# One ones-product instead of two for the adaLN parts that only one stream uses

## The chip, the cores and the metric

The kernel runs on one NeuronCore of a Trainium2 chip. Its engines are TensorE (PE in the profile, with its weight loads shown apart as PEld), VectorE (DVE), ScalarE (ACT), GpSimd (POOL) and SyncE (SP), which issues nearly all transfers. The metric is the time of one execution on the device in microseconds (us): the median of several runs.

## The reference

The model is a two-layer backbone over 512 latent tokens and 256 context tokens, 1024 wide. Layer 0 mixes tokens with gated linear attention (GLA), layer 1 with an mLSTM; each is followed by a convolutional feed-forward network (FFN). Around every block stands an adaptive norm: six vectors of 1024 per layer and stream (shift, scale and gate for the mixer, then for the FFN), made from a conditioning vector. Cut to what matters here:

```python
for i in range(DEPTH):                      # DEPTH = 2
    need_ctx = i < DEPTH - 1
    mod_l = (silu(c)     @ ada_w[i] + ada_b[i])[:, None, :]   # latent stream, 6*1024
    mod_c =  silu(c_ctx) @ ada_w[i] + ada_b[i]                # context stream, 6*1024
    sh1_l, sc1_l, g1_l, sh2_l, sc2_l, g2_l = split(mod_l, 6)
    sh1_c, sc1_c, g1_c, sh2_c, sc2_c, g2_c = split(mod_c, 6)
    h_c = rmsnorm(ctx, norm_mix_g[i]) * (1 + sc1_c) + sh1_c
    h_l = rmsnorm(x,   norm_mix_g[i]) * (1 + sc1_l) + sh1_l
    ...                                     # mixer
    x = x + g1_l * o_l
    h_l = rmsnorm(x, norm_ffn_g[i]) * (1 + sc2_l) + sh2_l
    x = x + g2_l * conv_ffn(h_l, ...)
    if need_ctx:                            # layer 0 only
        ctx = ctx + g1_c * o_c
        h_c = rmsnorm(ctx, norm_ffn_g[i]) * (1 + sc2_c) + sh2_c
        ctx = ctx + g2_c * conv_ffn(h_c, ...)
return rmsnorm(x, final_norm_g)
```

In layer 1 the context stream is not needed behind the mixer's input, so of its six parts only 0 and 1 are wanted for both streams, and parts 2 to 5 (`g1`, `sh2`, `sc2`, `g2`) for the latent stream alone.

## The kernel before

All activations stay on the chip, with the 1024 channels in eight tiles of 128 partitions. Every big product runs as three fp32r products of split operands (`mm3`, lines 384 to 386: high by high, low by high, high by low), each weight tile arriving as a 512 KB transfer into one of three "stage" buffers (`load_w`, line 362), being cast on ACT (line 340) and its remainder taken on DVE (line 341).

The program goes through a start, the GLA heads, FFN 0 (lines 1568 on), the four mLSTM heads and FFN 1. The instruction order on each engine is set when the program is built, by a scheduler that knows what depends on what; on the chip each engine then works down its own list in that order and waits where a semaphore asks for it.

The adaptive norm's vectors for all but the first two parts are made by the generator `ada_seq`, whose steps are woven into other work. A part is 1024 columns of `ada_w`, taken as two halves of 512 columns, and a half as eight blocks of 128 rows (`k` = 0 to 7). For each block there is one transfer of 256 KB (line 540, tile `ast`, three buffers, issued two steps ahead), and then one step of accumulation over the row blocks: ACT writes the first product into a fresh tile `asum` (line 555), DVE adds the others to it (line 558). The tile `asum` has two buffers. When the eighth block is in, TensorE sums over the 128 partitions by a product with a matrix of ones, 32 columns wide, so that four of them fill the four column groups of the array (line 567); ACT copies the result (line 569, tile `aev`), TensorE transposes it (line 572) and DVE adds the bias into `mod` (line 575 for two streams, line 581 for one).

Where both streams are needed, a half has two sums of 512 columns and the four products take 256 columns each, with a copy of 256 columns and two transposes. Where one stream is needed, a half has one sum, the four products take 128 columns each, with a copy of 128 columns and one transpose.

Who takes the steps: in FFN 0 one step is taken behind each projection from block 4 on (`project`); part 2 of layer 1 falls there, around blocks 15 to 18. In the mLSTM stage, parts 3 to 5 are the side work of a `Filler`: `ml_scan`, one head's chain of small dependent steps, alternates with projections of the next head, and every 1.9 us of such filling, by the filler's own reckoning, one step of `ada_seq` is let in, up to a number of steps that is given per head.

The head's chain (lines 1425 to 1507) matters below. For ten steps, TensorE transposes a block of keys (`mkp`, line 1458), ACT scales it (`mktok`, line 1460), TensorE makes a state update (`mu`, line 1465) and DVE folds it into the state (`C`, line 1471). All of `mkp`, `mu`, the head's later outputs `num` and the transposes `hps` of the head before take their PSUM space from one ring of three buffers (`aux`). After the chain DVE multiplies the decays with the scores (`Wt`, line 1489).

In tile names, the digits behind `ast1_` and `asum0_1_` are part, half and row block: `ast1_413` is part 4, half 1, block 3. The digits behind `C`, `mu` and `mkp` are head, direction and block.

Of the kernel before, what the change touches and what calls it, by code (L numbers as in the profile page):

```python
# [16 lines left out]
F32 = mybir.dt.float32  # L17
# [3 lines left out]
AF = mybir.ActivationFunctionType  # L21
ALU = mybir.AluOpType
PSUM = bass.MemoryType.PSUM

P = 128
D = 1024
KT = D // P
# [273 lines left out]
class Body:  # L301
# [226 lines left out]
    def ada_seq(self, parts):  # L528
# [5 lines left out]
        nc = self.nc  # L534
# [10 lines left out]
        for i, (l, part, half, k) in enumerate(steps):  # L545
# [6 lines left out]
            if k == 0:  # L552
                acc = [self.pw.tile([P, 512], F32, tag="ada_sum", name=f"asum{s}_{nm}", bufs=2) for s in range(len(c))]
                for s in range(len(c)):
                    nc.scalar.activation(acc[s], st, AF.Copy, scale=c[s])  # L555
            else:
                for s in range(len(c)):
                    nc.vector.scalar_tensor_tensor(acc[s], st, c[s], acc[s], op0=ALU.mult, op1=ALU.add)  # L558
            yield 0.0
            if k < KT - 1:  # L560
                continue

            ps = self.ada_tile(f"ada{nm}")
            n = 256 if both else 128
            for j in range(4):
                x = acc[j % 2][:, j // 2 * n:j // 2 * n + n] if both else acc[0][:, j * n:j * n + n]
                nc.tensor.matmul(ps[32 * j:32 * j + 32, 0:n], self.ones, x, start=True, stop=True)
            ev = self.pw.tile([P, 256], F32, tag="adaev", name=f"aev{nm}", bufs=1)
            nc.scalar.copy(ev[:, :n], ps[:, :n])
            yield n / 474  # L570
            for i_ in range(n // P):
                nc.tensor.transpose(ps[:, 256 + i_ * P:256 + (i_ + 1) * P], ev[:, i_ * P:(i_ + 1) * P], self.ident)
            b = part * KT + half * 4
            if both:
                nc.vector.tensor_tensor(
                    self.mod[l][:, b:b + 4, :].rearrange("p (q i) s -> p q i s", i=2),
                    ps[:, 256:512].rearrange("p (i q s x) -> p q i s x", i=2, q=2, x=32)[:, :, :, :, 0],
                    self.adab[l][:, b:b + 4].rearrange("p (q i) -> p q i", i=2).unsqueeze(3).to_broadcast([P, 2, 2, 2]),
                    op=ALU.add)
            else:  # L580
                nc.vector.tensor_tensor(self.mod[l][:, b:b + 4, 0], ps[:, 256:384:32], self.adab[l][:, b:b + 4], op=ALU.add)
            if half and part in (1, 4):
                self.make_A(l, part // 4, 0, KT, 2 if both else 1)
            yield n / 1164
# [946 lines left out]
    def mlstm(self):  # L1531
        with ExitStack() as es:
# [16 lines left out]
            with self.tc.tile_pool(name="ml_b", bufs=1) as hpb:  # L1549
# [6 lines left out]
                for h in range(NH):  # L1556
# [12 lines left out]
                    fill = Filler(*fill, side=ada((15, 19, 18, 8)[h]))  # L1569
# [265 lines left out]
```

## Time and profile before

| | |
|---|---|
| median of 3 runs | 1616.74 us (1615.61 to 1618.33) |
| the profiled execution's own time | 1618.06 us |
| its span, first to last instruction | 1616.0 us, granted TensorE clock 0.998 |
| TensorE busy | 1595.1 us (99%), 9249 instructions |
| weight loads busy | 1378.6 us (85%) |
| VectorE busy | 1232.0 us (76%) |
| ScalarE busy | 679.2 us (42%) |
| GpSimd busy | 67.4 us (4%) |
| moved | 163.59 MB, 101 GB/s over the span |

The profile comes from one execution, which took 1618.06 us, 2.06 us more than its span; sums are made against the span, and then carried over to the median. In a row of the timeline stand the start and the length in us, the engine, the line, the operation with out<-in, and the shape; in brackets the idle time of the engine just before it and what ended it. Since matmuls are pipelined, what one costs on TensorE is read from the distance of two starts, not from its length.

### The profile page before, as it was taken

Reading aid. Unit: us, or ns where it says so; the run is one execution under the profiler, and the core shown is the slowest. Engines: PE = TensorE matmul, PEld = TensorE weight load, DVE = VectorE, ACT = ScalarE, POOL = GpSimd, SP = SyncE. Lnnn points to the kernel's source line nnn. Section 1 sums busy time; section 2 is a strip of 40 time slices with the busy share of each in tenths; the row PEclk is TensorE's granted clock in tenths of the full one; section 3 lists DMA queues with packets and bytes.
Section 4 is the critical chain, followed back from the end, with each engine's and each line's share of the span. In section 5 each row is a group of like instructions: output and inputs, shape, how many; then the busy total and the mean of one; then the engine's idle time right before and its main releaser. Section 6 shows DMA issues by size and latency. Waiting matters only on the chain. (4 is left out here: it accounts for less than half of the span.)

```text
span 1616.0 us, 23563 instructions
## 1 busy us (share of the span) xinstructions
PE 1595.1 (99%) x9249; PEld 1378.6 (85%) x9249; DVE 1232.0 (76%) x2123; ACT 679.2 (42%) x1149; POOL 67.4 (4%) x128
## 2 busy tenths in 40 slices
PE   7999999999999999999999999999999999999998
PEld 6789898889888888888888988888889888888887
DVE  5776988878985978695755678766778988877875
ACT  5673738435431314131321356545465422323334
POOL 0110101011000000000000020000001000000000
PEclk9999999999999999999999999999999999999999
DMA  9613453432240524251312205433340423223421
GB/s 304 183 51 101 128 154 93 133 96 82 88 124 27 149 74 118 65 169 51 100 53 63 57 27 151 137 112 104 98 118 14 123 89 99 85 79 100 117 79 53
DMA packets 178674, 163.59 MB, mean 101 GB/s; under 512 B 8924, under 2 KB 146788, under 8 KB 178564
## 3 DMA queue, kind: packets, MB, share of 16 engines
q1 hardware_dynamic: 178324, 161.97, 33.4%
q8 instruction: 72, 1.18, 0.3%
q14 instruction: 38, 0.31, 0.1%
q10 hardware_dynamic: 240, 0.13, 0.0%
HBM read 159.98 MB, written 2.10 MB: 100 GB/s over the span
## 5 line engine op out<-in xcount | busy, mean ns | idle before, releaser
L1648 DVE SCALAR_TENSOR_TENSOR acc<-gp,vt_f,acc 128x512 f32<-128x512 f32 x352 | 260.4, 748 | 4.6
L558 DVE SCALAR_TENSOR_TENSOR asum<-ast,sil,asum 128x512 f32<-128x512 f32 x224 | 163.8, 754 | 20.9 <-ACT asum L555 11.3
L384 PE MATMUL fd<-ahil,wh_d 128*128 128x512 f32 (+1 forms) x376 | 142.1, 378 | 0.6 <-DVE xl L629 0.5
L386 PE MATMUL fd<-ahil,wl_d 128*128 128x512 f32 (+1 forms) x376 | 141.7, 378 | 0.0
L385 PE MATMUL fd<-alol,wh_d 128*128 128x512 f32 (+1 forms) x376 | 141.3, 376 | 0.0
L629 DVE SCALAR_TENSOR_TENSOR xl<-fd,mod,xl 128x512 f32<-128x512 f32 (+1 forms) x128 | 90.8, 715 | 55.7 <-PE fd L386 55.1
L384 PE MATMUL fa<-hhi,wh_a 128*128 128x512 f32 x320 | 124.9, 390 | 0.0
L384 PE MATMUL fg<-hhi,wh_g 128*128 128x512 f32 x320 | 124.8, 390 | 0.0
L385 PE MATMUL fg<-hlo,wh_g 128*128 128x512 f32 x320 | 124.5, 389 | 0.0
L386 PE MATMUL fg<-hhi,wl_g 128*128 128x512 f32 x320 | 124.5, 389 | 0.0
L386 PE MATMUL fa<-hhi,wl_a 128*128 128x512 f32 x320 | 124.5, 389 | 0.0
L385 PE MATMUL fa<-hlo,wh_a 128*128 128x512 f32 x320 | 124.5, 389 | 0.0
L1649 ACT ACTIVATE acc<-acc,vt_f 128x256 f32<-128x256 f32 (+1 forms) x66 | 43.1, 653 | 175.0 <-DVE acc L1648 174.7
L340 ACT CAST wh_a<-st_a 128x1024 fp32r<-128x1024 f32 x43 | 45.2, 1051 | 101.0 <-PE fg L385 86.7
L1632 ACT COPY gp<-fg 128x512 f32<-128x512 f32 x40 | 23.3, 582 | 146.1 <-PE fg L386 146.1
L384 PEld LDWEIGHTS fd<-ahil,wh_d 128*128 128x128 f32 x376 | 70.7, 188 | 14.4 <-DVE xl L629 1.9
L386 PEld LDWEIGHTS fd<-ahil,wl_d 128*128 128x128 f32 x376 | 70.6, 188 | 13.1 <-DVE wl_d L341 0.2
L385 PEld LDWEIGHTS fd<-alol,wh_d 128*128 128x128 f32 x376 | 70.7, 188 | 12.3
L340 ACT CAST wh_d<-st_d 128x1024 fp32r<-128x1024 f32 x44 | 45.9, 1051 | 76.4 <-PE fd L385 53.9
L341 DVE TENSOR_TENSOR wl_a<-st_a,wh_a 128x1024 fp32r<-128x1024 f32 x43 | 52.5, 1220 | 33.5 <-ACT wh_a L340 33.5
L386 PEld LDWEIGHTS fg<-hhi,wl_g 128*128 128x128 f32 x320 | 60.1, 188 | 12.6
L386 PEld LDWEIGHTS fa<-hhi,wl_a 128*128 128x128 f32 x320 | 60.0, 188 | 12.7
(1436 smaller groups left out, 4481.2 us busy)
## 6 DMA issues: line engine op xcount, KB each, us to landing
ast<-in_ada_w_dram SPq DMA_DIRECT2D x160, 256.0 KB
st_g<-in_ffn_w_up_dram SPq DMA_DIRECT2D x44, 512.0 KB
st_a<-in_ffn_w_up_dram SPq DMA_DIRECT2D x44, 512.0 KB
st_d<-in_ffn_w_down_dram SPq DMA_DIRECT2D x44, 512.0 KB
ast<-in_ada_w_dram SPq DMA_DIRECT2D x16, 512.0 KB
st_wo<-in_gla_w_out_dram SPq DMA_DIRECT2D x14, 512.0 KB
st_gr<-in_gla_w_in_dram SPq DMA_DIRECT2D x8, 512.0 KB
st_mo<-in_mlstm_w_in_dram SPq DMA_DIRECT2D x8, 512.0 KB
```

Source lines behind the costliest of these rows:

```text
L340: return (nc.scalar.copy(hi, src), (eng or nc.vector).tensor_tensor(lo, src, hi.bitcast(F32), op=ALU.subtract))
L341: (eng or nc.vector).tensor_tensor(lo, src, hi.bitcast(F32), op=ALU.subtract))
L384: nc.tensor.matmul(ps, wl[0], wr[0], start=start, stop=False)
L385: nc.tensor.matmul(ps, wl[0], wr[1], start=False, stop=False)
L386: nc.tensor.matmul(ps, wl[1], wr[0], start=False, stop=stop)
L558: nc.vector.scalar_tensor_tensor(acc[s], st, c[s], acc[s], op0=ALU.mult, op1=ALU.add)
L629: self.nc.vector.scalar_tensor_tensor(xv, ps, gate, xv, op0=ALU.mult, op1=ALU.add)
L1632: nc.scalar.copy(g[:, 1:ROWS + 1, 1:W_GRID + 1], ps[c0].rearrange("p (r w) -> p r w", r=ROWS))
L1648: nc.vector.scalar_tensor_tensor(o, s, tw, o, op0=ALU.mult, op1=ALU.add)
L1649: nc.scalar.activation(acc[:, c0:c0 + n], acc[:, c0:c0 + n], AF.Gelu_apprx_tanh, bias=cb[:, c:c + 1])
```

## The change

For the parts that one stream alone uses (parts 2 to 5 of layer 1), the two halves of a part are no longer finished one by one. Both halves' sums over the row blocks are kept, in the two `asum` buffers; only behind the sixteenth block come four ones-products, now of 256 columns each (two from each half's sum), one copy of 256 columns, two transposes, and one addition of the bias for all eight blocks of 128 columns. A part then has 18 steps in place of 20, and the numbers of steps per mLSTM head go from (15, 19, 18, 8) to (15, 18, 18, 8). The path of the parts that both streams use computes as before. (The lines behind it move down by 5 in the changed kernel: line 558 becomes 559, 572 becomes 573, 1471 becomes 1476.)

```diff
@@ ada_seq @@
             if k == 0:
-                acc = [self.pw.tile([P, 512], F32, tag="ada_sum", name=f"asum{s}_{nm}", bufs=2) for s in range(len(c))]
+                new = [self.pw.tile([P, 512], F32, tag="ada_sum", name=f"asum{s}_{nm}", bufs=2) for s in range(len(c))]
                 for s in range(len(c)):
-                    nc.scalar.activation(acc[s], st, AF.Copy, scale=c[s])
+                    nc.scalar.activation(new[s], st, AF.Copy, scale=c[s])
+                acc = new if both or not half else acc + new
             else:
                 for s in range(len(c)):
-                    nc.vector.scalar_tensor_tensor(acc[s], st, c[s], acc[s], op0=ALU.mult, op1=ALU.add)
+                    nc.vector.scalar_tensor_tensor(acc[s - len(c)], st, c[s], acc[s - len(c)], op0=ALU.mult, op1=ALU.add)
             yield 0.0
-            if k < KT - 1:
+            if k < KT - 1 or not (both or half):
                 continue
 
             ps = self.ada_tile(f"ada{nm}")
-            n = 256 if both else 128
             for j in range(4):
-                x = acc[j % 2][:, j // 2 * n:j // 2 * n + n] if both else acc[0][:, j * n:j * n + n]
-                nc.tensor.matmul(ps[32 * j:32 * j + 32, 0:n], self.ones, x, start=True, stop=True)
+                q, i_ = (j // 2, j % 2) if both else (j % 2, j // 2)
+                nc.tensor.matmul(ps[32 * j:32 * j + 32, 0:256], self.ones, acc[i_][:, q * 256:q * 256 + 256],
+                                 start=True, stop=True)
             ev = self.pw.tile([P, 256], F32, tag="adaev", name=f"aev{nm}", bufs=1)
-            nc.scalar.copy(ev[:, :n], ps[:, :n])
-            yield n / 474
-            for i_ in range(n // P):
+            nc.scalar.copy(ev, ps[:, :256])
+            yield 0.54
+            for i_ in range(2):
                 nc.tensor.transpose(ps[:, 256 + i_ * P:256 + (i_ + 1) * P], ev[:, i_ * P:(i_ + 1) * P], self.ident)
-            b = part * KT + half * 4
             if both:
+                b = part * KT + half * 4
                 ...
             else:
-                nc.vector.tensor_tensor(self.mod[l][:, b:b + 4, 0], ps[:, 256:384:32], self.adab[l][:, b:b + 4], op=ALU.add)
+                b = part * KT
+                nc.vector.tensor_tensor(
+                    self.mod[l][:, b:b + KT, 0].rearrange("p (q i) -> p q i", i=2),
+                    ps[:, 256:512].rearrange("p (i q x) -> p q i x", i=2, x=32)[:, :, :, 0],
+                    self.adab[l][:, b:b + KT].rearrange("p (q i) -> p q i", i=2), op=ALU.add)
             if half and part in (1, 4):
                 self.make_A(l, part // 4, 0, KT, 2 if both else 1)
-            yield n / 1164
+            yield 0.22
@@ mlstm @@
-                    fill = Filler(*fill, side=ada((15, 19, 18, 8)[h]))
+                    fill = Filler(*fill, side=ada((15, 18, 18, 8)[h]))
```

The change also moves instructions, since part 4's first sum can only begin where part 3's two buffers come free. First TensorE at the border of mLSTM heads 0 and 1, where part 3 is finished. `wic11` and `mub11` are rows of head 1's beginning, `vpsmv23` is a projection of head 2's values. Before, the place where the second half of part 3 is summed:

```order
L386 MATMUL vpsmv24_10166<-wh_mv24_10074,hlo_10_8678 128x256
L567 MATMUL ada1_31_10203<-asum0_1_31_9816,ones_66 32x128 x4
L384 MATMUL vpsmv25_10210<-wh_mv20_10068,hhi_10_8677 128x256
L385 MATMUL vpsmv25_10210<-wl_mv20_10069,hhi_10_8677 128x256
L386 MATMUL vpsmv25_10210<-wh_mv20_10068,hlo_10_8678 128x256
L1458 MATMUL mkp101_10214<-ident_61,kT1_9885 128x128
```

And now, where all of part 3 is:

```order
L1433 MATMUL wic11_10085<-mstk_9417,sel_9251 128x2
L385 MATMUL vpsmv23_10114<-wl_mv20_10058,hhi_10_8669 128x256
L386 MATMUL vpsmv23_10114<-wh_mv20_10057,hlo_10_8670 128x256
L567 MATMUL ada1_31_10131<-asum0_1_30_9506,ones_66 32x256 x2
L567 MATMUL ada1_31_10131<-asum0_1_31_9753,ones_66 32x256 x2
L384 MATMUL vpsmv23_10114<-wh_mv24_10063,hhi_10_8669 128x256
L385 MATMUL vpsmv23_10114<-wl_mv24_10064,hhi_10_8669 128x256
L386 MATMUL vpsmv23_10114<-wh_mv24_10063,hlo_10_8670 128x256
L384 MATMUL vpsmv23_10114<-wh_mv24_10063,hhi_10_8669 128x256
L1435 MATMUL mub11_10087<-mstk_9417,sel_9251 128x512
```

The ones-product of part 3 stood behind the first five instructions of head 1's chain; it stands now ahead of `mub11`, before the chain. The one that stood in head 0 for the first half is gone.

Next DVE in head 1's chain. Before, the first half of part 4 (`asum0_1_40`) has been accumulated during head 0, and the second half lies between the state updates:

```order
L558 SCALAR_TENSOR_TENSOR asum0_1_41_10595<-ast1_413_10623,sil_119,asum0_1_41_10595 128x512
L1471 SCALAR_TENSOR_TENSOR C102_10245<-C101_10188,dec10_10054,mu101_10243 128x257
L558 SCALAR_TENSOR_TENSOR asum0_1_41_10595<-ast1_414_10657,sil_119,asum0_1_41_10595 128x512
L558 SCALAR_TENSOR_TENSOR asum0_1_41_10595<-ast1_415_10669,sil_119,asum0_1_41_10595 128x512
L1471 SCALAR_TENSOR_TENSOR C114_10267<-C115_10220,dec11_10102,mu115_10265 128x257
L558 SCALAR_TENSOR_TENSOR asum0_1_41_10595<-ast1_416_10829,sil_119,asum0_1_41_10595 128x512
L1471 SCALAR_TENSOR_TENSOR C103_10294<-C102_10245,dec10_10054,mu102_10292 128x257
L558 SCALAR_TENSOR_TENSOR asum0_1_41_10595<-ast1_417_10856,sil_119,asum0_1_41_10595 128x512
L1471 SCALAR_TENSOR_TENSOR C113_10322<-C114_10267,dec11_10102,mu114_10320 128x257
L341 TENSOR_TENSOR wl_mo11_10432<-st_mo11_10429,wh_mo11_10431 128x1024
L845 SCALAR_TENSOR_TENSOR og00_9740<-hps1000_10344,vt_v1_82,og00_9740 128x512
L1471 SCALAR_TENSOR_TENSOR C104_10356<-C103_10294,dec10_10054,mu103_10354 128x257
```

Now both halves lie there:

```order
L1476 SCALAR_TENSOR_TENSOR C102_10227<-C101_10175,dec10_10043,mu101_10225 128x257
L559 SCALAR_TENSOR_TENSOR asum0_1_40_10206<-ast1_406_10327,sil_119,asum0_1_40_10206 128x512
L559 SCALAR_TENSOR_TENSOR asum0_1_40_10206<-ast1_407_10380,sil_119,asum0_1_40_10206 128x512
L1476 SCALAR_TENSOR_TENSOR C114_10255<-C115_10198,dec11_10091,mu115_10253 128x257
L559 SCALAR_TENSOR_TENSOR asum0_1_41_10447<-ast1_411_10415,sil_119,asum0_1_41_10447 128x512
L1476 SCALAR_TENSOR_TENSOR C103_10281<-C102_10227,dec10_10043,mu102_10279 128x257
L559 SCALAR_TENSOR_TENSOR asum0_1_41_10447<-ast1_412_10445,sil_119,asum0_1_41_10447 128x512
L559 SCALAR_TENSOR_TENSOR asum0_1_41_10447<-ast1_413_10469,sil_119,asum0_1_41_10447 128x512
L1476 SCALAR_TENSOR_TENSOR C113_10309<-C114_10255,dec11_10091,mu114_10307 128x257
L559 SCALAR_TENSOR_TENSOR asum0_1_41_10447<-ast1_414_10517,sil_119,asum0_1_41_10447 128x512
L341 TENSOR_TENSOR wl_mo11_10422<-st_mo11_10419,wh_mo11_10421 128x1024
L1476 SCALAR_TENSOR_TENSOR C104_10336<-C103_10281,dec10_10043,mu103_10334 128x257
```

Between `Wt11`'s preparation and the product `Wt10` of this chain, DVE's list now has 13 accumulations, two of them behind `C105`, where it had 7; one more stands behind `Wt11`. Head 2 shows the same with part 5. The transfers follow on SP's list. `ast1_403` to `ast1_407` stood ahead of the next four weight tiles, and now stand behind them. Before:

```order
L540 DMA ast1_402_10275<-in_ada_w_dram 128x512
L362 DMA st_mv24_10072<-in_mlstm_w_in_dram 128x4x256
L540 DMA ast1_403_10307<-in_ada_w_dram 128x512
L540 DMA ast1_404_10337<-in_ada_w_dram 128x512
L540 DMA ast1_405_10382<-in_ada_w_dram 128x512
L540 DMA ast1_406_10402<-in_ada_w_dram 128x512
L540 DMA ast1_407_10425<-in_ada_w_dram 128x512
L362 DMA st_mo10_10368<-in_mlstm_w_in_dram 128x8x128
```

Now:

```order
L540 DMA ast1_402_10204<-in_ada_w_dram 128x512
L362 DMA st_mv24_10061<-in_mlstm_w_in_dram 128x4x256
L362 DMA st_mo10_10358<-in_mlstm_w_in_dram 128x8x128
L362 DMA st_mo11_10419<-in_mlstm_w_in_dram 128x8x128
L362 DMA st_wo100_10497<-in_mlstm_w_out_dram 128x1024
L362 DMA st_wo101_10503<-in_mlstm_w_out_dram 128x1024
L540 DMA ast1_403_10235<-in_ada_w_dram 128x512
L540 DMA ast1_404_10266<-in_ada_w_dram 128x512
```

In FFN 0 the ones-product and the transpose of part 2's first half are gone, and those of the whole part stand behind the latent projection of block 18 (`fg018`); nothing else changes place on TensorE there.

## The prediction

> **What bounds the kernel now.** I read the page's busy times first, then busy time by stage (start, GLA, FFN 0, mLSTM, FFN 1; the columns behind the stretch are its length, then PE, PEld, DVE, ACT, POOL busy with instructions), then TensorE's waits in the mLSTM stage (total, times, longest).
>
> ```profile
> PE 1595.1 (99%) x9249; PEld 1378.6 (85%) x9249; DVE 1232.0 (76%) x2123; ACT 679.2 (42%) x1149; POOL 67.4 (4%) x128
> ...
> 420.00:820.00 400.00, 400.00 (x2323) 351.21 (x2322) 304.66 (x478) 107.64 (x164) 0.00 (x0) 1.00 0.31 93
> 820.00:1250.00 430.00, 427.82 (x2583) 375.75 (x2582) 307.28 (x640) 209.63 (x383) 21.96 (x57) 1.00 0.30 88
> ...
> PE wib L1425 <- DVE mstk L1339: 0.9, 1, 0.9
> PE hps L839 <- DVE og L845: 0.6, 1, 0.6
> ```
>
> In the two stages that the change touches, TensorE is idle for 0.00 and 2.18 us. So time falls only where TensorE's list gets shorter, and rises only where a change of order makes TensorE wait; what ACT and DVE save is worth nothing by itself. The wait of `hps` for `og` (0.6 us) shows how such a wait looks: a PSUM buffer of the `aux` ring that DVE had not yet read.
>
> **What the change removes from TensorE.** The same ones-product stands in FFN 0 in both sizes, between the same neighbours (end of a 512-column projection, beginning of a 256-column one): 128 columns in part 2, 256 columns in a part for two streams.
>
> ```profile
> 767.90 0.39 PE L385 MATMUL fg<-hlo,wh_g 128*128 128x512 f32 x1
> 768.12 0.39 PE L386 MATMUL fg<-hhi,wl_g 128*128 128x512 f32 x1
> ...
> 768.44 0.42 PE L567 MATMUL ada<-asum,ones 128*32 128x128 f32 x8
> ...
> 768.80 0.39 PE L384 MATMUL fg<-chi,wh_g 128*128 128x256 f32 x1
> ...
> 769.03 0.28 PE L385 MATMUL fg<-clo,wh_g 128*128 128x256 f32 x1
> ...
> 769.15 0.28 PE L386 MATMUL fg<-chi,wl_g 128*128 128x256 f32 x1
> ```
>
> ```profile
> 633.31 0.39 PE L386 MATMUL fg<-hhi,wl_g 128*128 128x512 f32 x1
> 633.63 0.64 PE L567 MATMUL ada<-asum,ones 128*32 128x256 f32 x8
> 634.20 0.39 PE L384 MATMUL fg<-chi,wh_g 128*128 128x256 f32 x1
> 634.43 0.28 PE L385 MATMUL fg<-clo,wh_g 128*128 128x256 f32 x1
> ```
>
> Undisturbed starts are 0.22 us apart at 512 columns (767.90 to 768.12) and 0.12 us at 256 (769.03 to 769.15), so the two neighbours alone take 0.34 us. From 768.12 to 769.03 it is 0.91 us: four products of 128 columns cost 0.57 us. From 633.31 to 634.43 it is 1.12 us: four of 256 columns cost 0.78 us. Twice the columns cost 0.21 us more, not twice as much; most of the price is the coming and going.
>
> ```profile
> 771.64 0.28 PE L386 MATMUL fg<-chi,wl_g 128*128 128x256 f32 x1
> 771.76 0.27 PE L572 MATMUL ada<-ident,aev 128*128 128x128 f32 x1
> 771.79 0.48 PE L384 MATMUL fa<-hhi,wh_a 128*128 128x512 f32 x1
> 772.11 0.40 PE L385 MATMUL fa<-hlo,wh_a 128*128 128x512 f32 x1
> ```
>
> ```profile
> 637.04 0.28 PE L386 MATMUL fg<-chi,wl_g 128*128 128x256 f32 x1
> 637.16 0.38 PE L572 MATMUL ada<-ident,aev 128*128 128x128 f32 x2
> 637.30 0.47 PE L384 MATMUL fa<-hhi,wh_a 128*128 128x512 f32 x1
> 637.61 0.39 PE L385 MATMUL fa<-hlo,wh_a 128*128 128x512 f32 x1
> ```
>
> In the same way one transpose costs 0.47 - 0.34 = 0.13 us and two cost 0.57 - 0.34 = 0.23 us. A part cost 2 x (0.57 + 0.13) = 1.40 us and will cost 0.78 + 0.23 = 1.01 us. That is 0.39 us for each of parts 2, 3, 4 and 5, together **1.56 us**. The price of the columns could be different among the small products of the mLSTM stage; bounds are no saving there (0.39 us from FFN 0 alone) and the whole of one ones-product and none of the column price (0.57 x 4 = 2.3 us).
>
> **What it removes elsewhere.** These are all 20 copies and the eight additions for one stream (ns are shortest, median, longest):
>
> ```profile
> L569 ACT COPY aev<-ada x20: 245/350/377, 121.2 to 1215.2; 128x256 f32<-128x256 f32 x12, 128x128 f32<-128x128 f32 x8
> ...
> L581 DVE TENSOR_TENSOR mod<-ada,vt_v x8: 151/155/164, 772.5 to 1221.2; 128x4 f32<-128x4 f32 x8
> ```
>
> ACT loses eight short copies and gains four long ones, some 8 x 0.25 - 4 x 0.36 = 0.6 us; DVE loses four additions, 0.6 us. Both engines have idle time behind TensorE's work in these stages (400.00 - 304.66 us on DVE in FFN 0), so I count them at nothing. Nothing waits early for `mod`: part 2 (`g1`) is still finished in FFN 0 and first used in head 1's output projection, and parts 3 to 5 are used behind the last head.
>
> **What it moves.** In FFN 0 the accumulations keep their places, and the one later product costs no wait. In the mLSTM stage it is different: both `asum` buffers are now held until a part is finished, so all 16 blocks of parts 4 and 5 fall into the chains of heads 1 and 2. On DVE's list 6 accumulations more stand ahead of `Wt` there; at 0.75 us each that is 4.5 us. These rows tell whether they fit (the first is DVE's share of head 1's chain, then its waits in it):
>
> ```profile
> 1053.00:1077.00 24.00, 23.44 (x164) 21.08 (x163) 13.57 (x23) 9.68 (x23) 0.64 (x1) 1.00 0.45 132
> ...
> DVE asum L558 <- ACT asum L555: 4.1, 1, 4.1
> DVE asum L558 <- DMA ast<-in_ada_w_dram: 3.3, 4, 2.1
> DVE Wt L1489 <- PE msp L1486: 1.9, 1, 1.9
> ```
>
> DVE has 10.4 us idle in those 24 us, so its work is covered. Its transfers are the question: DVE takes its list in order, so a state update `C` behind an accumulation whose block hasn't landed is late, its `aux` buffer is late, and TensorE stands at the next `mkp` or `mu`. How fast blocks come is read from a transfer's issue to the accumulation that waited for it:
>
> ```profile
> 1131.56 0.33 SPq L540 DMA_DIRECT2D ast<-in_ada_w_dram  x1
> 1134.41 0.75 DVE L558 SCALAR_TENSOR_TENSOR asum<-ast,sil,asum 128x512 f32<-128x512 f32 x1 [0.21 <-DMA ast<-in_ada_w_dram]
> ...
> 1134.24 0.33 SPq L540 DMA_DIRECT2D ast<-in_ada_w_dram  x1
> 1136.84 0.75 DVE L558 SCALAR_TENSOR_TENSOR asum<-ast,sil,asum 128x512 f32<-128x512 f32 x1 [0.62 <-DMA ast<-in_ada_w_dram]
> ```
>
> It is 2.85 and 2.60 us; with the accumulation a buffer goes round in about 3.5 us. The Trainium skill's page DMA: Bandwidth & Descriptors (Anatomy of one DMA) fits a transfer by 2.0 us plus bytes over 436 GB/s; for 256 KB that would be an estimate of 2.6 us, and a round of 3.4 us. The trace agrees with it at its quicker row.
>
> `ast1_414`, the last block ahead of `C104`, is the 13th of its part; three lie ready, ten have to come, in three buffers: 10 / 3 x 3.5 = 11.7 us. Where this starts and where it must be done:
>
> ```profile
> 1048.16 0.33 SPq L362 DMA_DIRECT2D st_wo<-in_mlstm_w_out_dram  x1
> ...
> 1049.16 0.40 PE L1430 MATMUL mub<-mstk,sel 128*128 128x512 f32 x1
> ...
> 1052.90 0.35 ACT L1460 ACTIVATE mktok<-mkp,mcol 128x128 f32<-128x128 f32 x1
> ...
> 1069.64 0.47 DVE L1471 SCALAR_TENSOR_TENSOR C<-C,dec,mu 128x257 f32<-128x257 f32 x1
> ```
>
> Part 3's product now stands ahead of `mub11` (1049.16), but ACT's first product of part 4 stands behind `mktok111` (1052.90) and a copy, so the round begins near 1054. The four weight tiles that now go ahead of `ast1_403` on SP don't hold it up: the last of them was issued at 1048.16 even behind the blocks. Then `ast1_414` is in by about 1066 and added by 1066.7, `wl_mo11` (1.2 us) follows, and `C104` runs near 1068. Before it ran at 1069.64, and TensorE arrives 0.8 us earlier by then (parts 2 and 3). So the ring just keeps up, with less than a microsecond to spare. The bounds per head: no wait at all, or even 0.6 us gained, since the two groups of `hps` transposes now stand together and the wait quoted above may go; and 4.8 us lost, from the slow round worked out under the first rival. Being near the quick end I take 0.2 us per head for it. There is a second, smaller wait: `mu111` now stands four matmuls and two transposes behind `mkp111` (about 0.7 us), while ACT has the copy of `aev` and `mktok` (0.35 us each) to do between them; I take 0.2 us for it, and the same in head 2. Together **0.8 us** given back.
>
> **The sum.** The profiled span 1616.0 - 1.56 + 0.8 = 1615.2 us; with the 2.06 us around it 1617.3 for that execution, whose own time (1618.06) was 1.3 us above the median. On the median of 1616.74 the change is the same, -0.76: **1616.0 us**. About 0.2% (3.2 us) is what a measurement of this kernel can tell from no change, so I expect "no change".
>
> **Rivals.** First, *slower: the block ring sets head 1's and 2's chains.* One block of the profile came much later:
>
> ```profile
> 1061.02 0.75 DVE L558 SCALAR_TENSOR_TENSOR asum<-ast,sil,asum 128x512 f32<-128x512 f32 x1
> ...
> 1064.35 1.12 SPq L540 DMA_DIRECT2D ast<-in_ada_w_dram  x1
> ...
> 1066.78 0.75 DVE L558 SCALAR_TENSOR_TENSOR asum<-ast,sil,asum 128x512 f32<-128x512 f32 x1 [2.06 <-DMA ast<-in_ada_w_dram]
> ```
>
> `ast1_417` uses the buffer of `ast1_414` (1061.02), was issued only at 1064.35 by an instruction of 1.12 us, and made that round 5.76 us. If all rounds were so long, the ten blocks would take 19.2 us, `ast1_414` would be added near 1074, and `C104` would come 4.8 us late by the old clock: 9.6 us for two heads. For it: DVE's strict order, blocks that used to be taken in head 0's idle time. Against it: that round shared the queue with 512 KB weight tiles, which now go ahead. It decides by my 0.2% from a round of about 4.5 us (10 / 3 x 1.0 us more, 3.3 us per head, less the microsecond to spare, twice: 4.7 - 1.56 = 3.1). A middle case of 3 us per head gives **1621.2 us**. The Trainium skill's page Trainium Kernel Development and Optimization (Best Practices) asks for double buffers so that transfers and work overlap; the change gives that up for the sums, and by this rule the time would go this way. Chance 0.12.
>
> Second, *all of it arrives*: the ring keeps up, no wait: 1616.74 - 1.56 = **1615.2 us**. For it: DVE's 10.4 us idle, 1.9 of them at the end of the chain. Against: the short margin. Chance 0.30.
>
> Third, *more than the sum*: full saving of 2.3 us, and the `hps` wait gone in both heads, 1.2 us: **1613.2 us**. Only one such wait is in the trace. Chance 0.08.
>
> Fourth, *the change doesn't shorten TensorE's list in the mLSTM stage*, where small products stand next to the ones-products anyway: -0.39 + 0.8, **1617.2 us**. Chance 0.05.
>
> **How the numbers follow.** The forecast has 0.45. The third rival's half and more lies beyond -0.2%: faster 0.07. The first is slower: 0.12. Within 0.2%: 0.81. The range reaches from the third rival's edge to a ring wait of 2.5 us per head (1616.74 - 1.56 + 5.0 = 1620.2): **1613.0 to 1620.2 us**.
>
> **What would show it.** Right: ones-products at 0.78 us between starts, four fewer groups; TensorE's idle time in the mLSTM stage within a microsecond of 2.18; DVE waiting for `ast` more than 3.3 us in head 1's chain without TensorE waiting for `C` or `og`. Wrong: TensorE rows of `mkp`, `mu` or `num` released by `C` or `Wt`, some microseconds together; or `ast` rounds above 4.5 us in heads 1 and 2.

## The result and the profile after

The changed kernel takes **1619.13 us** (median of 17 runs, 1617.95 to 1620.99), the kernel before 1616.04 us beside it (17 runs, 1615.37 to 1618.33). The ratio is 1.002 with a 95% interval of 1.0013 to 1.0026: 3.1 us slower, where no change was forecast. The profiled execution took 1618.55 us, with a span of 1616.6 us.

First the profile after: the page's busy times, then busy time of FFN 0 and of the mLSTM stage, then TensorE's waits in that stage.

```profile
PE 1594.3 (99%) x9217; PEld 1377.3 (85%) x9217; DVE 1232.3 (76%) x2119; ACT 674.2 (42%) x1143; POOL 68.1 (4%) x128
...
420.00:820.00 400.00, 400.00 (x2322) 351.66 (x2322) 303.41 (x477) 108.14 (x165) 0.00 (x0) 1.00 0.31 92
820.00:1250.00 430.00, 425.69 (x2534) 372.72 (x2532) 306.10 (x632) 203.48 (x375) 20.74 (x56) 1.00 0.30 88
...
PE mkp L1463 <- DVE C L1476: 2.0, 2, 1.4
PE wib L1430 <- DVE mstk L1344: 1.0, 1, 1.0
PE mu L1470 <- DVE og L850: 0.7, 2, 0.3
```

TensorE's list is shorter (1594.3 us busy against 1595.1), and TensorE stands 4.31 us in the mLSTM stage where it stood 2.18. The two new rows are the ones that the prediction named as signs of its first rival: `mkp` waits for `C`, `mu` for `og`. The old wait of `hps` for `og` is gone.

To see where the time went, the four heads are measured on TensorE, from the first `wib` of a head to that of the next, and from head 3's to the first row of the last projection `po130A`. The first and the last of these rows before:

```profile
996.66 0.47 PE L1425 MATMUL wib<-mstk,sel 128*128 128x512 f32 x1 [0.92 <-DVE mstk L1339]
...
1224.88 0.28 PE L384 MATMUL po130A<-hhi,wo_xc 128*128 128x256 f32 x1
```

And after:

```profile
994.71 0.47 PE L1430 MATMUL wib<-mstk,sel 128*128 128x512 f32 x1 [0.99 <-DVE mstk L1344]
...
1225.90 0.28 PE L384 MATMUL po130A<-hhi,wo_xc 128*128 128x256 f32 x1
```

The stretch of all four is 228.22 us before and 231.19 after (the heads start 1.95 us earlier in the second profile, 1.3 of it gained between 18 and 32 us, where the profile before shows a granted clock of 0.73, 0.50, 0.50 and 0.56 in the four microseconds from 19 to 23 and that after 1.00; lengths taken later don't suffer from that, but the two spans can't be compared as they are). By the prediction's prices it should have become 228.22 - 3 x 0.39 = 227.05 us. So **4.1 us** have to be found in the heads. The same stretches for every kernel that was run, each from its one profiled execution, with the times (a product of a part that moves over a head's border moves 0.7 or 1.0 us with it; the sum is free of that). Each ratio is against the kernel before beside it on the same chip, whose median lay between 1615.64 and 1616.58 us there, so small differences are read from the ratios:

| kernel | head 0 | head 1 | head 2 | head 3 | sum | median, us | ratio (95%) |
|---|---|---|---|---|---|---|---|
| before | 48.01 | 70.63 | 69.94 | 39.64 | 228.22 | 1616.04 | 1 |
| after | 47.37 | 71.82 | 70.95 | 41.05 | 231.19 | 1619.13 | 1.0020 (1.0013 to 1.0026) |
| five block buffers | 46.67 | 70.34 | 71.96 | 41.02 | 229.99 | 1618.53 | 1.0015 (1.0006 to 1.0024) |
| part 4's sums apart | 47.37 | 72.33 | 69.44 | 41.07 | 230.21 | 1619.44 | 1.0017 (1.0008 to 1.0026) |
| steps (18, 18, 18, 8) | 48.36 | 69.94 | 70.97 | 39.01 | 228.28 | 1616.83 | 1.0001 (0.9992 to 1.0010) |
| part 2 alone | 47.98 | 69.86 | 69.94 | 39.64 | 227.42 | 1615.12 | 0.9994 (0.9985 to 1.0003) |
| no transfers | 47.41 | 69.56 | 69.42 | 41.07 | 227.46 | 1615.65 | 0.9997 (0.9988 to 1.0006) |
| GpSimd adds | 47.40 | 76.66 | 80.61 | 41.05 | 245.72 | 1633.69 | 1.0107 (1.0093 to 1.0121) |
| steps (26, 18, 10, 8) | 48.35 | 70.45 | 69.50 | 39.00 | 227.30 | 1614.63 | 0.9992 (0.9983 to 1.0001) |
| before, steps (28, 20, 12, 8) | 48.59 | 74.67 | 70.37 | 39.00 | 232.63 | 1618.72 | 1.0015 (1.0006 to 1.0024) |
| steps (24, 18, 12, 8) | 48.36 | 69.79 | 69.52 | 39.01 | 226.68 | 1614.93 | 0.9991 (0.9982 to 1.0000) |
| steps (26, 18, 10, 8), five block buffers | 47.63 | 70.02 | 69.50 | 39.03 | 226.18 | 1615.04 | 0.9994 (0.9985 to 1.0003) |
| steps (26, 18, 10, 8), again | 48.36 | 70.55 | 69.50 | 38.99 | 227.40 | 1615.98 | 0.9996 (0.9987 to 1.0005) |
| steps (24, 18, 12, 8), again | 48.37 | 69.79 | 69.51 | 38.96 | 226.63 | 1614.95 | 0.9992 (0.9983 to 1.0002) |

Now the place in head 1. TensorE, after:

```profile
1067.30 0.40 PE L386 MATMUL mo<-hhi,wl_mo 128*128 128x512 f32 x1
1069.14 0.33 PE L1463 MATMUL mkp<-ident,kT 128*128 128x128 f32 x1 [1.45 <-DVE C L1476]
1069.80 0.70 PE L1470 MATMUL mu<-mvt,mktok 128*128 128x257 f32 x2 [0.33 <-DVE og L850]
1070.15 0.58 PE L384 MATMUL mo<-hhi,wh_mo 128*128 128x512 f32 x1
1070.57 0.39 PE L385 MATMUL mo<-hlo,wh_mo 128*128 128x512 f32 x1
```

DVE ahead of that wait, the last accumulation (`ast1_414`), a weight's remainder and `C104`:

```profile
1066.80 0.75 DVE L559 SCALAR_TENSOR_TENSOR asum<-ast,sil,asum 128x512 f32<-128x512 f32 x1 [0.96 <-DMA ast<-in_ada_w_dram]
1067.47 1.22 DVE L341 TENSOR_TENSOR wl_mo<-st_mo,wh_mo 128x1024 fp32r<-128x1024 f32 x1
1068.61 0.48 DVE L1476 SCALAR_TENSOR_TENSOR C<-C,dec,mu 128x257 f32<-128x257 f32 x1
```

`mkp` starts 0.05 us behind the end of `C104` (1069.09). And the transfers of one of the three buffers, `ast1_403`, `ast1_406`, `ast1_411` and `ast1_414`:

```profile
1051.90 0.33 SPq L540 DMA_DIRECT2D ast<-in_ada_w_dram  x1
...
1055.60 0.33 SPq L540 DMA_DIRECT2D ast<-in_ada_w_dram  x1
...
1059.29 0.33 SPq L540 DMA_DIRECT2D ast<-in_ada_w_dram  x1
...
1062.77 0.33 SPq L540 DMA_DIRECT2D ast<-in_ada_w_dram  x1
```

DVE's waits for all `ast` in this chain (total, times, longest):

```profile
DVE asum L559 <- DMA ast<-in_ada_w_dram: 4.4, 7, 1.0
```

The rounds are 3.70, 3.69 and 3.48 us, close to the 3.5 us that were assumed. Yet `ast1_414` is used only at 1066.80, 14.9 us behind the first issue, and added by 1067.55. DVE stood 4.4 us for blocks in the chain.

### The profile page after: what moved, and what is told of

It reads as the page before. It is cut to its first block, busy times and chain, and to the rows that moved or that the text cites. A ratio compares the mean times of both kernels' runs of the same rounds, so it can differ in the third digit from the quotient of the medians.

```text
span 1616.6 us, 23497 instructions
## 1 busy us (share of the span) xinstructions
PE 1594.3 (99%) x9217; PEld 1377.3 (85%) x9217; DVE 1232.3 (76%) x2119; ACT 674.2 (42%) x1143; POOL 68.1 (4%) x128
## 5 line engine op out<-in xcount | busy, mean ns | idle before, releaser
L559 DVE SCALAR_TENSOR_TENSOR asum<-ast,sil,asum 128x512 f32<-128x512 f32 x224 | 164.0, 755 | 20.6 <-DMA ast<-in_ada_w_dram 11.7
L386 PE MATMUL fd<-ahil,wl_d 128*128 128x512 f32 (+1 forms) x376 | 141.8, 378 | 0.0
L385 PE MATMUL fd<-alol,wh_d 128*128 128x512 f32 (+1 forms) x376 | 141.4, 376 | 0.0
L385 PE MATMUL fg<-hlo,wh_g 128*128 128x512 f32 x320 | 124.6, 389 | 0.0
L386 PE MATMUL fa<-hhi,wl_a 128*128 128x512 f32 x320 | 124.6, 389 | 0.0
L386 PE MATMUL fg<-hhi,wl_g 128*128 128x512 f32 x320 | 124.6, 389 | 0.0
L385 PE MATMUL fa<-hlo,wh_a 128*128 128x512 f32 x320 | 124.5, 389 | 0.0
L386 PEld LDWEIGHTS fd<-ahil,wl_d 128*128 128x128 f32 x376 | 70.6, 188 | 13.0 <-DVE wl_d L341 0.2
L385 PEld LDWEIGHTS fd<-alol,wh_d 128*128 128x128 f32 x376 | 70.7, 188 | 12.4
L386 PEld LDWEIGHTS fa<-hhi,wl_a 128*128 128x128 f32 x320 | 60.1, 188 | 12.6
L386 PEld LDWEIGHTS fg<-hhi,wl_g 128*128 128x128 f32 x320 | 60.1, 188 | 12.5
```

Of the source, the lines that this page charges most:

```text
L385: nc.tensor.matmul(ps, wl[0], wr[1], start=False, stop=False)
L386: nc.tensor.matmul(ps, wl[1], wr[0], start=False, stop=stop)
L559: nc.vector.scalar_tensor_tensor(acc[s - len(c)], st, c[s], acc[s - len(c)], op0=ALU.mult, op1=ALU.add)
```

## The experiments

Three theories stood against each other: **A**, the blocks come too slowly through three buffers, and DVE's strict order hands their lateness to `C`; **B**, the accumulations themselves are too much work for DVE in the chain; **C**, TensorE's list or its order costs the time, whatever DVE does.

**Five block buffers.**

```diff
-            st = self.pw.tile([P, 512], F32, tag="ada_w", ...)
+            n = (part * 2 + half) * KT + k
+            if more and n % 5 > 2:            # more: quarters of the tile xc
+                st = more[n % 5 - 1]
+            else:
+                st = self.pw.tile([P, 512], F32, tag="ada_w", ...)
```

> The changed kernel with one thing more: in the mLSTM stage the block ring has five buffers in place of three (two quarters of the tile `xc`, which is free by then). The sums stay as they are, so DVE still has 13 accumulations of parts 4 and 5 ahead of `Wt` in heads 1 and 2. Theory A (three buffers bring the blocks too slowly: in the profile of the changed kernel the thirteen `ast` issues of head 1 run from 1051.90 to 1067.58, 1.3 us apart, and `C` behind them holds up `mkp`): the waits `mkp` for `C` (1.4 and 0.5 us) and those behind them go, 1615.0 to 1617.0 us. Theory B (the six more accumulations themselves, 4.5 us of DVE per chain, make `C` late, whatever their transfers do): the waits stay, 1618.5 us or more. Theory C (TensorE's shorter list of small products doesn't save time in the mLSTM stage, or its new order costs it): 1618 to 1619 with the waits for `C` gone.

1618.53 us, 1.0015 (1.0006 to 1.0024): the time is that of theory B, and of C, but the waits fit none of the three as expected. Head 1 became 1.5 us shorter and its wait for `C` is gone; head 2 became 1.0 us longer:

```profile
1136.41 0.60 PE L1474 MATMUL mu<-mvt,mktok 128*128 128x257 f32 x2
1138.14 1.09 PE L848 MATMUL hps<-ident,mlo 128*128 128x128 f32 x8 [1.13 <-DVE C L1480]
```

DVE's order was not the same (TensorE's was, in heads 1 to 3): the build, which knows of the deeper ring, put all 14 of DVE's accumulations of part 5 ahead of the last three `C` of head 2, where the changed kernel has 10 there. Two of them waited for their blocks all the same, one for 1.46 us:

```profile
1134.31 0.75 DVE L563 SCALAR_TENSOR_TENSOR asum<-ast,sil,asum 128x512 f32<-128x512 f32 x1 [1.46 <-DMA ast<-in_ada_w_dram]
```

In head 1 all 14 stand ahead of the last four `C`, and no `C` is waited for. So head 1 speaks for A, and the run as a whole doesn't decide.

**Part 4's sums in tiles of their own.**

```diff
+                if more and part == 4:
+                    new = [more[half]]        # and no tile of ada_sum for part 4
```

> The changed kernel with part 4's two sums in tiles of their own (quarters of `xc`), so that part 4 need not wait for part 3's product: in DVE's list all accumulations of part 4 then stand ahead of head 1's chain, while those of part 5 stay in head 2's chain as in the changed kernel. Theory A (the ring) and theory B (DVE's work) both expect head 1's waits (`mkp` for `C` 1.4 us, `mu` for `og` 0.3 us, and what follows from them) to go and head 2's (0.5 and 0.3 us) to stay: 1616.3 to 1617.5 us. Theory C (TensorE's list or order): the waits in head 1 go but the time stays above 1618.

1619.44 us, 1.0017 (1.0008 to 1.0026): a miss for A and B alike, and the time of C, though not with the waits that C expects. The waits went from head 2 (69.44 us, no wait) and stayed in head 1 (72.33 us). TensorE's waits from head 1 to head 3:

```profile
PE mkp L1465 <- DVE C L1478: 0.9, 1, 0.9
PE wic L1435 <- DVE Wt L1450: 0.7, 1, 0.7
PE mu L1472 <- DVE og L852: 0.3, 1, 0.3
```

With both pairs of buffers free, part 4 moved ahead of head 1's chain, and the build drew 11 accumulations of part 5 forward into head 1's chain. Head 2's chain had none left and no wait. The waits for `C` and `og` follow the accumulations, not the part. The wait of `wic` for `Wt` is new, and its cause stays open: the last accumulation of part 4 ended at 1035.9 us, and the decay products of head 1 began only at 1047.4.

**Steps (18, 18, 18, 8).**

```diff
-                    fill = Filler(*fill, side=ada((15, 18, 18, 8)[h]))
+                    fill = Filler(*fill, side=ada((18, 18, 18, 8)[h]))
```

> The changed kernel with the numbers of steps per head (18, 18, 18, 8) in place of (15, 18, 18, 8), so that a part ends with its head: part 3 is summed over the partitions at the end of head 0, and the first three blocks of part 4 stand ahead of head 1's chain, 11 accumulations in place of 13 between its first decay products and `Wt`; the same in head 2. Theory A: with the blocks some 4 us further on, no wait for `C` in heads 1 and 2, and the whole saving arrives but for a few tenths: 1614.3 to 1615.8 us. Theory B: 11 accumulations instead of 13 take off a third of the surplus over 7: 1617.5 to 1618.5. Theory C: 1617.5 or more with no such waits.

1616.83 us, 1.0001 (0.9992 to 1.0010): 2.3 us better than the changed kernel by the medians (3.1 by the ratios), no better than before, and between the times that A and B expect. No wait for `C` is left, as theory A and not theory B expects, but a new one ahead of head 2's chain:

```profile
PE wic L1433 <- DVE Wt L1448: 0.9, 1, 0.9
```

There DVE's list has seven accumulations of part 5 between the scores of head 1 and the decay products of head 2, and one of them waited 0.98 us for its block; that this is what held up `Wt` is read from the order, not tested. Head 3 took 39.01 us, 2.04 us less than after, of which the moved product is 1.0.

**Part 2 alone.** The joint sum only where FFN 0 has it (`joint = part in (2,) and not both`, everything else as before).

> The kernel before, with part 2 alone (the one in FFN 0) summed over the partitions together, parts 3 to 5 half by half as before, steps (15, 19, 18, 8). By the prices of the FFN 0 rows (two times 0.57 + 0.13 us before, 0.78 + 0.23 us now) TensorE's list is 0.39 us shorter, with no wait added: 1615.6 us, ratio 0.9998. If the price of columns doesn't turn into time even in the stage where TensorE never waits: 1616.0.

1615.12 us, 0.9994 (0.9985 to 1.0003): not told apart from no change, and in keeping with the 0.39 us. In the profile TensorE's list runs 1.38 us ahead of before's in front of part 2 and 1.70 us behind it, so 0.32 us of it arrive. The heads' stretch is 227.42 us on the same lists as before, 0.8 us shorter: the wait of `hps` for `og` that before's profile has is not in this one.

**No transfers.** Parts 4 and 5 fetch two blocks of each half and use the second again.

```diff
+            if l == 1 and part > 3 and k > 1:
+                return ahead[-1]
             st = self.pw.tile([P, 512], F32, tag="ada_w", ...)
```

> The changed kernel, with part of the work left out: of parts 4 and 5 only the first two blocks of each half are fetched, and the accumulations of the other six take the second block again, so `mod` of these parts is not the reference's. DVE's list then has 14 accumulations ahead of the last four `C` in head 1's chain (the changed kernel has 10 ahead of the last three), and none of them but the first can wait for a transfer. Theory A (the transfers through three buffers make `C` late): no wait for `C` or `og` in heads 1 and 2, 1616 to 1617 us. Theory B (DVE's own work for the accumulations makes `C` late): the waits grow, since 14 stand where 10 stood (4 x 0.75 = 3.0 us more ahead of the last `C`, less the 4.4 us that DVE stood idle for transfers there): `mkp` waiting for `C` 1 us or more in head 1 and in head 2, 1618.5 to 1621 us.

1615.65 us, 0.9997 (0.9988 to 1.0006), 3.5 us less than the changed kernel by the medians: a little under the 1616 to 1617 us that A expects, and far from B's. Heads 1 and 2 are 3.8 us shorter, and their waits are gone, although DVE does all 14 accumulations of a part ahead of the last four `C` in each, where the changed kernel has 11 in head 1 and 10 in head 2 ahead of the last three. TensorE's rows at the same place of head 1:

```profile
1067.48 0.40 PE L386 MATMUL mo<-hhi,wl_mo 128*128 128x512 f32 x1
1067.71 0.27 PE L1465 MATMUL mkp<-ident,kT 128*128 128x128 f32 x1
1067.82 0.65 PE L1472 MATMUL mu<-mvt,mktok 128*128 128x257 f32 x2
...
1068.55 0.39 PE L385 MATMUL mo<-hlo,wh_mo 128*128 128x512 f32 x1
```

From L386 to L385 it is 1.07 us here and was 3.27 us after: 2.2 us in this place alone, more than the two waits of 1.45 and 0.33 us in brackets. TensorE's instructions stand in the same order in both kernels through all four heads. Laid beside each other, the two lists part by 2.2 us here, by 0.2 us at a `mu` in head 2 and by 1.3 us at the `mkp` and `mu` that wait there, and by less than a tenth at any other place. On DVE, the last two of 14 accumulations and the `C` that TensorE waited for:

```profile
1062.73 1.53 DVE L561 SCALAR_TENSOR_TENSOR asum<-ast,sil,asum 128x512 f32<-128x512 f32 x2
...
1066.59 0.48 DVE L1478 SCALAR_TENSOR_TENSOR C<-C,dec,mu 128x257 f32<-128x257 f32 x1
```

All the accumulations are done by 1064.3, and `C104` comes at 1066.59. Theory B is ruled out, and for heads 1 and 2 theory C too, since the order that it blames is unchanged; theory A holds for heads 1 and 2. The transfers as such are thereby the cause; that it is the ring of three buffers which makes them late is shown for head 1 by the run with five, which takes away 1.5 of its 2.3 us.

**GpSimd adds.**

```diff
+                    if l == 1 and part > 3:
+                        nc.gpsimd.tensor_scalar(st, st, c[s], None, op0=ALU.mult)
+                        nc.gpsimd.tensor_tensor(acc[s - len(c)], acc[s - len(c)], st, op=ALU.add)
+                    else:
                         nc.vector.scalar_tensor_tensor(...)
```

> The changed kernel with the accumulations of parts 4 and 5 taken off DVE: GpSimd multiplies the block in place by the coefficient and adds it to the sum. DVE's list has no accumulation at all in heads 1 and 2; TensorE's list and the transfers stay. If DVE's list is the carrier of the loss (theories A and B alike): the waits of `mkp` for `C` and `mu` for `og` in heads 1 and 2 are gone (in the changed kernel the two clusters of small products around them cost 2.3 and 1.35 us more than their kind does elsewhere), and 1615.3 to 1616.8 us is left, the rest of the loss being in head 3, where the ones-product of part 5 is split by `wic` (1.5 us from neighbour to neighbour in place of 0.9). If the loss is TensorE's own order (theory C): 1618 or more.

1633.69 us, 1.0107 (1.0093 to 1.0121): the largest miss, and useful. DVE no longer carries the lateness, ACT does: the first product of a half stands in ACT's list, waits for its block, and `mktok` stands behind it. TensorE's largest wait:

```profile
PE mu L1474 <- ACT mktok L1469: 7.3, 2, 4.4
```

ACT's rows there:

```profile
1067.14 0.72 ACT L555 ACTIVATE asum<-ast,sil 128x512 f32<-128x512 f32 x1 [7.54 <-DMA ast<-in_ada_w_dram]
1067.77 0.35 ACT L1469 ACTIVATE mktok<-mkp,mcol 128x128 f32<-128x128 f32 x1
```

And GpSimd's two groups (line, operation, shapes | busy us, mean ns | idle before):

```profile
L560 POOL TENSOR_SCALAR ast<-ast,sil 128x512 f32<-128x512 f32 x28 | 49.7, 1775 | 8.8 <-DMA ast<-in_ada_w_dram 8.7
L561 POOL TENSOR_TENSOR asum<-asum,ast 128x512 f32<-128x512 f32 x28 | 36.2, 1293 | 6.0 <-issue 2.9 <-POOL Wt L1456 1.0
```

GpSimd holds a buffer for 1.78 + 1.29 = 3.07 us where DVE holds it for 0.75, so the ring turns far more slowly. Theory A had to be put more widely: any engine that works down its list in order and has a block to wait for there is a carrier.

**Steps (26, 18, 10, 8).** The table of the changed kernel, half a part earlier.

> The changed kernel with steps (26, 18, 10, 8) per head: half a part earlier than in the run with (18, 18, 18, 8). In DVE's list all but two blocks of part 5 then stand between head 1's chain and head 2's, half of part 4 ahead of head 1's chain, and no ones-product stands in a chain or is split. All theories in which the loss comes from accumulations inside a chain: no wait for `C`, `og` or `Wt` in heads 1 to 3, the whole saving arrives, 1614.2 to 1615.6 us, ratio 0.9985 to 0.9995. If the saving of the column groups doesn't arrive in the mLSTM stage even so (theory C): 1616.0 to 1617.

1614.63 us, 0.9992 (0.9983 to 1.0001). The waits for `C` and `og` are gone, one of 0.4 us of `wic` for `Wt` is left in head 1. Run again:

> The kernel with steps (26, 18, 10, 8) once more, on the chip of these runs, for a narrower interval: 1614.2 to 1615.2 us, ratio 0.9988 to 0.9996.

1615.98 us, 0.9996 (0.9987 to 1.0005): outside the expected time, with nearly the same stretch in the heads (227.40 us). The same kernel, measured twice, thus differs by 1.4 us in its medians and by 0.0004 in its ratios. With five block buffers:

> The changed kernel with steps (26, 18, 10, 8) and five block buffers in the mLSTM stage (two of them quarters of `xc`). If what is left in (26, 18, 10, 8) comes from blocks that are waited for (DVE stood 4.0 us for `ast` there, and `wic` 0.4 us for `Wt`): 1613.8 to 1614.6 us. If the build only uses the deeper ring to put more accumulations ahead of `Wt` and into the chain, as it did in the run with five buffers alone: 1614.6 or more.

1615.04 us, 0.9994 (0.9985 to 1.0003), heads 226.18 us: the stretch is shorter and the wait of `wic` is gone, but the time is not told apart from that with three buffers.

**The kernel before, with its steps moved forward.**

```diff
-                    fill = Filler(*fill, side=ada((15, 19, 18, 8)[h]))
+                    fill = Filler(*fill, side=ada((28, 20, 12, 8)[h]))
```

> The kernel before, parts summed half by half, with its steps moved forward in the same way: (28, 20, 12, 8) in place of (15, 19, 18, 8), 28 being one part of 20 and 8 blocks. A control for the run with steps (26, 18, 10, 8): does the step table alone bring the gain? DVE's list then has 14 accumulations in head 1's chain (7 before) and none in head 2's. Where accumulations in a chain are the cause, it is them and not the joint sum that cost: `mkp` or `mu` waits of 1 to 2.5 us in head 1, none in head 2, 1616.5 to 1618.5 us. If the joint sum itself is the cause: 1616.3 as before.

1618.72 us, 1.0015 (1.0006 to 1.0024), just above the 1616.5 to 1618.5 us that the theory of accumulations in a chain expects, and with the wait in the head that has 14 of them. (The profiled execution is the slowest of the eleven, 1621.03 us, so its 74.67 us in head 1 need not be typical.)

```profile
1068.56 0.27 PE L1458 MATMUL mkp<-ident,kT 128*128 128x128 f32 x1
1070.64 0.70 PE L1465 MATMUL mu<-mvt,mktok 128*128 128x257 f32 x2 [1.81 <-DVE C L1471]
```

So the joint sum over the partitions isn't itself the cause: half by half, a slowness of the same kind can be made with a table of steps, and with the joint sum it can be unmade:

**Steps (24, 18, 12, 8).**

> The changed kernel with steps (24, 18, 12, 8). Between the tables (18, 18, 18, 8), which left a wait of `wic` for `Wt` in head 2, and (26, 18, 10, 8), which left one of 0.4 us in head 1 and puts the ones-products of parts 4 and 5 next to `mkp` and `mu`: here they stand between a chain and its outputs, all of part 5 is accumulated between head 1's chain and head 2's, and 9 accumulations of part 4 stand in head 1's chain. With the cause as found (blocks waited for inside a chain): no wait for `C`; some tenths at most for `Wt`: 1614.2 to 1615.4 us.

1614.93 us, 0.9991 (0.9982 to 1.0000). TensorE's waits in the mLSTM stage are down to the three that have nothing to do with the parts:

```profile
PE wib L1430 <- DVE mstk L1344: 1.0, 1, 1.0
PE vpsmv L386 <- POOL hlo L341: 0.3, 1, 0.3
PE po134A L384 <- DVE xl L634: 0.3, 1, 0.3
```

> The kernel with steps (24, 18, 12, 8) once more, for a narrower interval. In its profile the four heads' stretch on TensorE took 226.7 us, 1.5 us less than before: 1614.3 to 1615.3 us, ratio 0.9986 to 0.9994.

1614.95 us, 0.9992 (0.9983 to 1.0002). This version is about 4.2 us faster than the changed kernel by the medians, and 4.5 to 4.7 by the ratios. Against the kernel before, both medians are lower, by 1.5 and 0.7 us, but each interval reaches up to no change.

## Why the prediction was wrong

**The saving was priced rightly.** In FFN 0 after, the joint product stands between the same kind of neighbours:

```profile
824.55 0.39 PE L386 MATMUL fg<-hhi,wl_g 128*128 128x512 f32 x1
824.87 0.64 PE L567 MATMUL ada<-asum,ones 128*32 128x256 f32 x8
...
825.67 0.28 PE L385 MATMUL fg<-clo,wh_g 128*128 128x256 f32 x1
```

From 824.55 to 825.67 it is 1.12 us, 0.78 us without the neighbours, as computed. Over part 2 as a whole TensorE's list gains 0.32 us on before's (1.66 us ahead in front of it, 1.98 behind it), where 0.39 was forecast. In the mLSTM stage it shows where nothing stands in its way: with steps (24, 18, 12, 8) the heads take 226.68 us (226.63 in its second run), 0.7 us less than the 227.42 us of the run with part 2 alone, where three times 0.39 are 1.17. By these profiles the fourth rival is refuted in direction; about 0.4 us of the saving didn't show even there.

**The step that failed is the ring's "just keeps up, with less than a microsecond to spare"**, and in it "10 / 3 x 3.5 = 11.7 us". Mechanism, place and engines were seen; but they were given to the first rival, with a chance of 0.12, and the forecast went by a ring that keeps up. The term was mis-sized by a count. Three buffers that lie ready are all taken, so the tenth block to come is the fourth in its buffer: it is issued after three whole rounds, and then has to land and be added, which makes four rounds, 14.0 us at the assumed 3.5. Measured, three rounds were 10.87 us (1051.90 to 1062.77), the landing 4.03 (to 1066.80) and the addition 0.75: 15.65 us. So 2.3 of the 3.95 us that were missing are the count, 0.4 the rounds and 1.3 the last landing, which took 4.03 us where 2.60 to 2.85 had been read; why that one took so long stays open. The estimate by the Trainium skill's page DMA: Bandwidth & Descriptors (Anatomy of one DMA), 2.6 us, is below this row too; the page fits it to transfers issued by GpSimd, and these are issued by SyncE.

Where the change first acts, in front of part 2, TensorE's list runs 1.66 us ahead of before's in the profile after. `C104` came at 1068.61, which is 1070.27 by the old clock: 2.3 us later than the 1068 of the prediction and too late for TensorE, which stood 1.45 us for it. The rest of the 3.95 us was hidden chiefly by two things: the prediction began at 1054, where it was 1053.6 by that clock, and it put the last addition once more behind the 11.7 us. With whole rounds, and the same prices, `C104` would have been put between 1069.3 and 1070.3 us, 0.5 to 1.5 us too late for TensorE, according to whether that addition is counted twice; with that in each of two heads, and the 0.4 us kept for the other wait, the forecast would have been 1616.5 to 1618.5 us. So the count alone makes lateness the likely case, but it does not give its whole size. The price that was given, 0.2 us per head (0.4 with the second wait), was 2.3 us in head 1 and 1.5 us in head 2 by their stretches (71.82 against 69.56 and 70.95 against 69.42 us without transfers).

That 1619.13 us lies within the stated 1613.0 to 1620.2 us is no success of the sum: the range reached so far by allowing for ring waits of 2.5 us per head, the case that the forecast had put aside.

**The rival's own size was wrong as well.** It asked for rounds of more than 4.5 us; the rounds were 3.5 to 3.7. Its 4.8 us per head for the slow round doesn't follow from its own terms either: added near 1074, with `wl_mo11` behind it as in the forecast, the block would put `C104` near 1075.2, 5.6 us behind 1069.64.

**`mkp` to `mu`.** 0.2 us per head were given to ACT between the two at the chain's beginning; no wait is seen there. What came is 0.33 us in each head at a later `mu`, from `og` on DVE. The groups of `hps` now stand together, as was said, and the wait of `hps` for `og` did go. But `og` stands right behind `C104` in DVE's list (1069.00), and without transfers this wait of `mu` is gone too, so it is a second face of the late block.

**Head 3 wasn't priced at all.** It became 1.41 us longer. The product of part 5 now lies there whole, 1.01 us in place of half a part's 0.70. A further 0.6 us is read from its rows:

```profile
1189.78 0.40 PE L386 MATMUL mo<-hhi,wl_mo 128*128 128x512 f32 x1
1190.10 0.62 PE L567 MATMUL ada<-asum,ones 128*32 128x256 f32 x2
1190.65 0.27 PE L1433 MATMUL wic<-mstk,sel 128*128 128x2 f32 x1
1190.85 0.63 PE L567 MATMUL ada<-asum,ones 128*32 128x256 f32 x6
...
1191.75 0.40 PE L385 MATMUL mo<-hlo,wh_mo 128*128 128x512 f32 x1
```

From L386 to L385 it is 1.97 us; two 512-column projections take 0.46 and `wic` alone some 0.1 (1190.41 to 1190.98 before, with two projections, is 0.57), which leaves 1.40 us for the four products that cost 0.78 together elsewhere: one of them stands on the other side of `wic`, so it seems that their coming and going is paid twice. The remaining 0.5 us lies among the small products of head 3's chain, whose order changed; it was not traced further.

**The account.** 227.05 us expected, 3.8 in heads 1 and 2 (the run without transfers takes them away), 1.1 in head 3, less 0.8 for the wait that only before's profile has: 231.15, measured 231.19. Shown by a run is the cause in heads 1 and 2; the 0.6 us in head 3 is read from rows, and no run was made for it alone (with steps (18, 18, 18, 8), where no product lies in head 3, that head is 1.0 us shorter beyond the product's own price). The two medians differ by 3.1 us; heads and part 2 together give 2.97 - 0.32 = 2.65 in the profiles, and the rest isn't traced.

## What to carry to other kernels

Count a ring of buffers in whole rounds, plus the landing and the use of the last block: a fraction of a round doesn't exist, and a margin smaller than one transfer is no margin to build a forecast on. Side work that waits for transfers does no harm where its engine idles, and holds up everything behind it where the engine's list is a chain of small dependent steps; so a change that ties buffers together longer is to be judged by where the freed work can go next, and the table that places it belongs to the change. When an experiment alters what the build knows (more buffers, other engines), compare the lists before the times: two of the runs here tested another order than was meant.

## What had not been expected of the hardware

After a wait of 1.81 us (and a second of 0.40 us close behind it) TensorE was granted half its clock for some 3 us. This is the kernel before with steps (28, 20, 12, 8), in two stretches behind that wait (the third number from the right is the granted clock):

```profile
1071.00:1072.00 1.00, 1.00 (x5) 0.53 (x3) 1.00 (x2) 0.00 (x0) 0.00 (x0) 1.00 0.55 147
1073.00:1074.00 1.00, 1.00 (x5) 0.90 (x4) 1.00 (x2) 0.03 (x1) 0.00 (x0) 0.50 0.74 187
```

The projections there:

```profile
1073.77 0.63 PE L385 MATMUL mo<-hlo,wh_mo 128*128 128x512 f32 x1
1074.20 0.63 PE L386 MATMUL mo<-hhi,wl_mo 128*128 128x512 f32 x1
```

Two 512-column products stand 0.43 us apart there, 0.23 elsewhere; 3 us at about half the pace are some 1.5 us more, nearly the wait's own length. In the changed kernel the clock stayed at 1.00 in the mLSTM stage, through its wait of 1.45 us. The length of a wait alone doesn't decide it: at the kernel's start TensorE stands 1.15 us for ACT in both profiles, and the clock then fell to 0.50 before (from about 19.5 to 22.9 us) and stayed at 1.00 after. The Trainium skill's page TensorE: Matmul & The Clock Gate (Why this matters for your kernels) warns of idle gaps above some 3 us; here a start-to-start gap of 2.08 us (1068.56 to 1070.64) came ahead of it, so to stay under the page's limit was not enough here; where the limit lies, these runs don't show.

GpSimd took about 1.78 us for a product of 128x512 with a column of coefficients and about 1.29 us for an addition of the same size, where DVE does both in one operation of 0.75 us.
